# Hybrid SSD and attention layer: the two directions of the state recurrence as two lanes, with four staging tiles

## The chip, the cores and the metric

The kernel runs on one NeuronCore of a Trainium2 chip. The metric is the device time of one execution in microseconds (us), taken as the median over runs. A trace of one profiled execution stands beside the times.

## What is computed

The reference is one encoder layer over 1024 tokens of width 1024. A LayerNorm of the input `h` feeds one input projection; its columns go to two parallel groups, and an output projection with a residual LayerNorm ends the layer. The change touches the first group alone, a Mamba-2 state-space group (SSD) in two head groups `g` of 8 heads each, run forward and backward in time:

```python
def ssd_chunked(x, dt, A, Bm, Cm):          # one direction, chunks of 128 tokens
    ...
    chunk_states = jnp.einsum("bclgn,bclgjp->bcgjpn", Bm, xdt * decay_to_end[..., None])
    def step(h, inp):
        st, dec = inp
        return dec[..., None, None] * h + st, h
    _, prev = lax.scan(step, h0, ...)
    y_off = jnp.einsum("bclgn,bcgjpn->bclgjp", Cm, prev) * jnp.exp(a_cs)[..., None]
    return (y_diag + y_off).reshape(b, s, g, j, p)
...
y_fwd = ssd_chunked(xf, dtf, A_f, Bf, Cf)
y_bwd = flip(ssd_chunked(flip(xf), flip(dtb), A_b, flip(Bf), flip(Cf)))
y = y_fwd + y_bwd + D * xf
...
y_ssm = rms_norm(y * silu(z), ssm_norm_g)
```

The scan over the 8 chunks is the state recurrence. The forward and the backward one do not depend on each other; they add into the same `y`.

## The kernel before, in words

**A planner orders the work.** The kernel is written as generators, called lanes, that a class `Loom` (lines 47 to 127) runs while the program is built. Each lane issues some instructions and yields the tiles that its next instruction needs. The loom keeps a model of time for each engine: `_pe_cost`, `_dve_cost` and `_pool_cost` (lines 175 to 209) price an instruction, and `slot` (line 85) places it in the first gap of its engine's modelled calendar. `run` (line 103) resumes the lane whose tiles are ready first on that model, a margin added, and among lanes that are equally ready the one of lowest rank. Ranks and margins stand in line 29: `states=(4.4, 0.8)`, `diag=(4.125, 0.6)`, `maps=(4.4, 0.6)`, `gate=(4.375, 0.2)`, `fill=(9, 0.8)`. So the projection's matmuls (`fill`) go where nothing else is ready. TensorE's instructions keep the order in which the lanes issued them (`pinned=True`, line 227): when the model was too optimistic, TensorE waits in front of that instruction and everything behind it waits as well.

**The projection.** `fill` (line 328) takes 52 blocks of 128 columns from a queue, each of 48 matmuls of 128x512, its weights split into a high and a low part (`whi` by ScalarE, `wlo` by GpSimd, line 291). The blocks before the attention are b and c of group 0, x of group 0, z of group 0, x, b and c of group 1, z of group 1, and q, k and v of the first attention head.

**The group's lanes.** `ssd(g)` (line 697) adds four lanes. `states` (line 706) turns b into tokens, computes the products `cb`, starts the output tiles `yt` from `xt` by `start_y` (line 731, four chunks at once, the other four inside the loop), and then runs the recurrence (lines 738 to 766): backward (`d` = 1), and when all its 8 chunks are done forward (`d` = 0). One step is, in order: VectorE makes the weighted input `xw`; TensorE multiplies the state `H[d]` by c into a PSUM bank (`sb`); GpSimd decays the state, `H <- H*dec`; VectorE scales the bank into `tm`; GpSimd adds `yt <- yt + tm`; TensorE multiplies `xw` by b into another bank; VectorE adds that, `H <- H + bank`. Each group has 14 matmul pairs, 14 additions on GpSimd and 12 decays. `xw` and `tm` have two buffers each, and `tm` is shared with `tmd` (line 724) and the gate's `ys` (line 850).

`maps` (line 770) loads 16 pairs of tiles `t`, and ScalarE and VectorE (`copy_predicated`, line 797) turn each into decays; `diag` (line 804) multiplies it by `cb` on VectorE, has TensorE multiply it by `xt`, and adds the result to `yt` on VectorE. `gate` (line 824) takes a chunk when all 8 diagonal parts of its half and the forward pass of that chunk are done (`gr.fwd > c`, line 835). When the last chunk of group 0 is through, and group 1's x, b and c are there, `ssd(1)` is added; when group 1's gate is through, the attention's tiles are opened (line 972) and its lanes start.

The block c of group 1 enters the projection when `G[0].fwd == NCH` (line 863).

Of the kernel before, what the change touches and what calls it, by code (L numbers as in the profile page):

```python
# [9 lines left out]
F32 = mybir.dt.float32  # L10
# [11 lines left out]
NCH = 8  # L22
# [9 lines left out]
def col_bcast(ap, n):  # L32
    return ap.unsqueeze(len(ap.shape)).broadcast_to(list(ap.shape) + [n])
# [183 lines left out]
def hybrid_layer_kernel(  # L217
# [8 lines left out]
    loom = Loom(tc)  # L226
    T = Engine(loom, nc.tensor, "PE", _pe_cost, pinned=True)
    V = Engine(loom, nc.vector, "DVE", _dve_cost)
    A = Engine(loom, nc.scalar, "ACT", _act_cost)
    P = Engine(loom, nc.gpsimd, "POOL", _pool_cost)  # L230
# [6 lines left out]
    def open_pool(stack, name, under=(), **kw):  # L237
        return Pool(loom, stack.enter_context(tc.tile_pool(name=name, bufs=1, **kw)), under, kw.get("space") != PSUM)
# [45 lines left out]
    def stage_w(col, i, pool, bufs):  # L284
        st = pool.tile([128, 4, 128], F32, name="wst", bufs=bufs)
        return st, w_in[512 * i:512 * i + 512, col:col + 128].rearrange("(k p) n -> p k n", p=128)
# [9 lines left out]
    class Block:  # L296


        def __init__(self, col, evac, when=None, after=None):
            self.col, self.evac, self.when, self.after = col, evac, when, after  # L300
            self.w, self.begun = [], 0
            self.pair = self.last = False
# [73 lines left out]
    def sbank(shape=(128, 512)):  # L376
        return s_p.tile(shape, F32, name="sb", bufs=4)
# [3 lines left out]
    dts, acs, nacs, ef, dec, wend = [  # L381
        sp.tile([128, 2, NCH, 16], F32, name=n) for n in ("dts", "acs", "nacs", "ef", "dec", "wend")]
# [3 lines left out]
    class Group:  # L386
        def __init__(self):
            self.x_done = 0
            self.bc = {}
            self.z_done = 0  # L390
            self.fwd = 0
            self.diag = [0, 0]
            self.gate = self.started = 0
            self.prepared = False
            self.q = []

    G = [Group(), Group()]
# [45 lines left out]
    def bc_block(g, name, when=None):  # L443
        def after(dst):
            G[g].bc[name] = dst
            return
            yield
        conv_block((8 if name == "b" else 10) + g, when,
                   lambda: sp.tile([128, S], F32, name=name + "_ch"), after)
# [33 lines left out]
    with tc.tile_pool(name="dp", bufs=1) as dp_, tc.tile_pool(name="p0", bufs=1) as p0_:  # L483
# [178 lines left out]
        for i in range(2):  # L662
            for b in queue[:2]:
                st, src = stage_w(b.col, i, p0, 4)
# [29 lines left out]
    yl = late["yl"] = open_pool(sx, "yl", (dp, p0))  # L694
    sq = late["sq"] = open_pool(sx, "sq", (dp, p0))

    def ssd(g):
        gr = G[g]
        hs = slice(8 * g, 8 * g + 8)
        cb = []  # L700
        env = {}

        def heads(t):
            return t.rearrange("p (h e) -> p h e", h=8)

        def states():
            yield lambda: gr.x_done == 4 and len(gr.bc) == 2
            xt, b_ch, c_ch = gr.xt, gr.bc["b"], gr.bc["c"]
            b_tok = yl.tile([128, NCH, 128], F32, name="b_tok")
            yt = env["yt"] = [yl.tile([128, 4, 512], F32, name=f"yt{h}") for h in range(2)]  # L710
            H = [yl.tile([128, 512], F32, name=f"H{d}") for d in range(2)]
            yield from to_tokens(b_ch, lambda half, pt: A.copy(b_tok[:, 4 * half:4 * half + 4, :], pt))
            dg = yl.tile([128, NCH], F32, name="dg")
            dc = yl.tile([128, NCH, 8], F32, name="dc")
            for half in range(2):
                pt = bank((128, 4, 128))
                yield (c_ch, pt)
                for j in range(4):
                    t = slice(128 * (4 * half + j), 128 * (4 * half + j) + 128)
                    T.matmul(pt[:, j, :], b_ch[:, t], c_ch[:, t], start=True, stop=True)  # L720
                m = yl.tile([128, 4, 128], F32, name="cb", bufs=2)
                A.copy(m, pt)
                cb.append(m)
                tm = sq.tile([128, 4, 128], F32, name="tmd", tag="tm", bufs=2)
                V.tensor_mul(tm, pt, ident.unsqueeze(1).broadcast_to([128, 4, 128]))
                V.tensor_reduce(dg[:, 4 * half:4 * half + 4], tm, axis=mybir.AxisListType.X, op=ALU.add)
            gr.prepared = True
            V.tensor_mul(dc, dts[:, 1, :, hs], col_bcast(dg, 8))
            V.tensor_add(dc, dc, d_skip[:, hs].unsqueeze(1).broadcast_to([128, NCH, 8]))

            def start_y(c, eng):
                eng.tensor_mul(heads(yt[c // 4][:, c % 4, :]), heads(xt[c // 4][:, c % 4, :]),
                               col_bcast(dc[:, c, :], 64))
                gr.started += 1

            for c in range(7, 3, -1):
                start_y(c, V if c % 2 else P)
            for d in (1, 0):
                order = range(NCH) if d == 0 else range(NCH - 1, -1, -1)
                for i, c in enumerate(order):  # L740
                    xc, yc = xt[c // 4][:, c % 4, :], yt[c // 4][:, c % 4, :]
                    if d == 1 and c < 4:
                        start_y(c, V if c % 2 else P)
                    if i < NCH - 1:
                        xw = sq.tile([128, 512], F32, name="xw", bufs=2)
                        V.tensor_mul(heads(xw), heads(xc), col_bcast(wend[:, d, c, hs], 64))
                    if i > 0:
                        po = sbank()
                        yield (H[d], po)
                        T.matmul(po, c_ch[:, 128 * c:128 * c + 128], H[d], start=True, stop=True)  # L750
                        efc = col_bcast(ef[:, d, c, hs], 64)
                        if i < NCH - 1:
                            P.tensor_mul(heads(H[d]), heads(H[d]), col_bcast(dec[:, d, c, hs], 64))
                        tm = sq.tile([128, 512], F32, name="tm", tag="tm", bufs=2)
                        V.tensor_mul(heads(tm), heads(po), efc)
                        P.tensor_add(yc, yc, tm)
                    if i < NCH - 1:
                        pss = sbank()
                        yield (xw, pss)
                        T.matmul(pss, b_tok[:, c, :], xw, start=True, stop=True)  # L760
                        if i == 0:
                            A.copy(H[d], pss)
                        else:
                            yield (H[d], pss)
                            V.tensor_add(H[d], H[d], pss)
                    gr.fwd += 1 - d

        order = [(1, h) for h in range(4)] + [(0, h) for h in range(8)] + [(1, h) for h in range(4, 8)]

# [54 lines left out]
        def gate():  # L824
            gz = {}

            def load(c):
                gz[c] = sq.tile([128, 512], F32, name="gz", bufs=2)
                dma(gz[c], zd[g][c])
            yield lambda: gr.z_done == 8  # L830
            load(0)
            load(1)
            for c in range(NCH):
                half = c // 4
                yield lambda: gr.diag[half] == 8 and gr.fwd > c
                y = env["yt"][half][:, c % 4, :]
                ms = sq.tile([128, 1], F32, name="ms", bufs=2)
                V.tensor_mul(y, y, gz[c])
                A.activation(gz[c], y, AF.Square, accum_out=ms)
                if c + 2 < NCH:  # L840
                    load(c + 2)
                V.tensor_scalar(ms, ms, 1.0 / 512, EPS, op0=ALU.mult, op1=ALU.add)
                P.tensor_tensor(ms, ms, mhalf, op=ALU.pow)
                yield ms
                V.tensor_scalar(y, y, ms, None, op0=ALU.mult)
                pt = bank((128, 4, 128))
                yield (y, pt)
                for b in range(4):
                    transpose(pt[:, b, :], y[:, 128 * b:128 * b + 128])
                ys = sq.tile([128, 4, 128], F32, name="ys", tag="tm", bufs=2)  # L850
                V.tensor_mul(ys, pt, col_bcast(cols[:, c_sg + 4 * g:c_sg + 4 * g + 4], 128))
                dma(y_dram[c][:, 4 * g:4 * g + 4, :], ys)
                gr.gate += 1
# [6 lines left out]
    for j in range(4):  # L860
        x_block(1, j)
    bc_block(1, "b", lambda: G[0].prepared)
    bc_block(1, "c", lambda: G[0].fwd == NCH)
    for j in range(4):
        z_block(1, j)
    ssd(0)
# [452 lines left out]
```

## Time and profile before

| | us |
|---|---|
| median of 3 runs | 1234.8 |
| lowest and highest run | 1231.69, 1235.98 |
| the profiled execution's own time | 1231.77 |
| its span from first to last instruction | 1230.1 |

Almost all instructions are recorded under line 140, the helper that every engine call goes through, so groups are told apart by the tiles that they write and read: `sb` is a bank of the states lane, `bk` a bank of everything else, `hh`, `hl`, `whi` and `wlo` belong to the projection, `xt` with `t` to the diagonal parts. PE is TensorE, DVE is VectorE, ACT is ScalarE, POOL is GpSimd. One fp32 product of 128x512 shows as two matmul rows. The recurrence of group 0 lies at 128 to 203 us of the span, that of group 1 at 300 to 376 us. Busy times in the view by stretches count time once; the sums of single durations can be larger, because successive instructions of an engine overlap at their ends.

### The profile page before, as it was taken

The numbers are of one execution on the slowest core, as the hardware profiler recorded it, in microseconds if no ns is written. First come the engines' busy times: TensorE is split into PE (matmuls) and PEld (weight loads), VectorE is DVE, ScalarE is ACT, GpSimd is POOL, SyncE is SP. The second block draws the span as 40 slices with busy tenths as digits, with TensorE's granted clock in tenths as the row PEclk, the third lists the DMA queues.
The fourth block names the chain that finished last, engine by engine and source line by source line (L and its number), as shares of the span: only waits on it lengthen the run. The fifth ranks groups of instructions, "written<-read, shape, count | busy, mean of one in ns | idle before, by whom it ended". The sixth has DMA issues, their size and how long they took to land. (4 is left out here: it accounts for less than half of the span.)

```text
span 1230.1 us, 16472 instructions
## 1 busy us (share of the span) xinstructions
PE 1173.1 (95%) x5881; PEld 920.5 (75%) x5881; DVE 898.5 (73%) x1303; ACT 701.8 (57%) x1281; POOL 471.2 (38%) x404
## 2 busy tenths in 40 slices
PE   5999999999999999999999999999999997999997
PEld 3777667788668777778787777877777776788885
DVE  6686876767876568788788887887878888762334
ACT  4557578734577466566655657556656686552221
POOL 7412564323753223323332333233232429352354
PEclk9999999999899999999999999999999999999999
DMA  6113345622344531111111121121111263023221
GB/s 199 30 36 112 86 129 158 185 64 65 94 122 144 153 113 43 28 47 48 26 48 39 43 53 26 35 52 36 43 35 43 79 210 116 26 77 121 78 86 60
DMA packets 107590, 98.02 MB, mean 80 GB/s; under 512 B 9364, under 2 KB 79349, under 8 KB 107509
## 3 DMA queue, kind: packets, MB, share of 16 engines
q1 hardware_dynamic: 107509, 96.98, 27.4%
q8 instruction: 46, 0.75, 0.3%
q14 instruction: 35, 0.29, 0.1%
HBM read 75.85 MB, written 16.91 MB: 75 GB/s over the span
## 5 line engine op out<-in xcount | busy, mean ns | idle before, releaser
L140 PE MATMUL bk<-hh,whi 128*128 128x512 f32 x832 | 352.8, 424 | 0.9 <-DVE yt L140 0.3
L140 PE MATMUL bk<-hl,whi 128*128 128x512 f32 x832 | 327.2, 393 | 3.2 <-POOL hl L140 2.8
L140 PE MATMUL bk<-hh,wlo 128*128 128x512 f32 x832 | 328.2, 394 | 0.0
L140 ACT ACTIVATE p<-p,nm 128x1024 f32<-128x1024 f32 x128 | 146.8, 1148 | 127.7 <-DVE nm L140 126.9
L140 POOL TENSOR_TENSOR wlo<-wst,whi 128x512 fp32r<-128x512 f32 x104 | 159.0, 1534 | 144.6 <-ACT whi L140 122.2
L140 POOL TENSOR_SCALAR p<-p,rs 128x1024 f32<-128x1024 f32 x56 | 64.4, 1150 | 352.7 <-DVE rs L140 293.0
L140 PEld LDWEIGHTS bk<-hh,wlo 128*128 128x128 f32 x832 | 156.7, 188 | 35.0
L140 PEld LDWEIGHTS bk<-hh,whi 128*128 128x128 f32 x832 | 157.6, 189 | 33.1 <-issue 5.7
L140 PEld LDWEIGHTS bk<-hl,whi 128*128 128x128 f32 x832 | 157.8, 190 | 32.8 <-POOL hl L140 5.5
L140 DVE CUSTOM_DVE_ANT_0 p<-sc,dist 128x1024 f32<-128x1024 f32 x128 | 151.3, 1219 | 20.2 <-PE sc L140 19.6
L140 DVE SCALAR_TENSOR_TENSOR p<-p,rs,p 128x1024 f32<-128x1024 f32 x64 | 127.7, 1995 | 21.3 <-POOL p L140 18.0
L140 ACT CAST wh<-bk 128x512 fp32r<-128x512 f32 x128 | 74.2, 580 | 50.5 <-PE bk L140 49.9
L140 DVE TENSOR_TENSOR wl<-bk,wh 128x512 fp32r<-128x512 f32 x128 | 87.1, 684 | 15.6 <-ACT wh L140 13.6
L140 ACT CAST whi<-wst 128x512 fp32r<-128x512 f32 x104 | 64.1, 621 | 42.5 <-PE bk L140 34.3
L140 PE MATMUL bk<-ident,p 128*128 128x128 f32 x512 | 78.3, 275 | 2.6 <-ACT o L140 2.2
L140 PEld LDWEIGHTS bk<-ident,p 128*128 128x128 f32 x512 | 61.0, 140 | 26.1 <-issue 5.5
L140 ACT ACT_TABLE_LOAD x46 | 59.0, 1283 | 28.9 <-DVE t L140 17.3
L140 PE MATMUL bk<-wh,vh 128*128 128x256 f32 x256 | 74.7, 292 | 0.0
L140 PE MATMUL sc<-kk,q 128*128 128x512 f32 x256 | 72.3, 394 | 0.0
L140 PE MATMUL bk<-wl,vh 128*128 128x256 f32 x256 | 72.0, 281 | 0.0
L140 PE MATMUL bk<-wh,vl 128*128 128x256 f32 x256 | 72.0, 281 | 0.0
L140 PEld LDWEIGHTS bk<-xt,t 128*128 128x128 f32 x256 | 45.0, 190 | 24.7 <-issue 16.0
(217 smaller groups left out, 2161.3 us busy)
## 6 DMA issues: line engine op xcount, KB each, us to landing
wst<-in_w_in_dram SPq DMA_DIRECT2D x104, 256.0 KB, 3.0
t<-acs_d SPq DMA_DIRECT2D x64, 256.0 KB, 3.4
ws<-in_w_out_dram SPq DMA_DIRECT2D x32, 256.0 KB, 3.8
ys<-yd SPq DMA_DIRECT2D x32, 256.0 KB, 3.0
xb<-in_x_dram SPq DMA_DIRECT2D x8, 512.0 KB, 6.5
zd<-zs SPq DMA_DIRECT2D x16, 256.0 KB, 3.0
gz<-zd SPq DMA_DIRECT2D x16, 256.0 KB, 3.1
yd<-ys SPq DMA_DIRECT2D x16, 256.0 KB, 2.8
```

The lines of the kernel that those rows point to most:

```text
L140: r = f(*args, **kw)
```

## The change

Each direction becomes a lane of its own, `chain(d, ...)`, both added to the loom under the name `states` (same rank and margin) after the four first `start_y`. A chunk's `start_y` is issued by whichever lane reaches the chunk first; the set `begun` keeps it from being issued twice, so there are still eight. `xw` and `tm` (with `tmd` and `ys`, which share its buffers) get four buffers in place of two. The gate and block c of group 1 wait for counters of both directions. Nothing is added to or taken from the arithmetic, and the lanes issue no DMA.

```diff
-            self.fwd = 0
+            self.done = [0, 0]
...
-                tm = sq.tile([128, 4, 128], F32, name="tmd", tag="tm", bufs=2)
+                tm = sq.tile([128, 4, 128], F32, name="tmd", tag="tm", bufs=4)
...
             for c in range(7, 3, -1):
-                start_y(c, V if c % 2 else P)
+                start_y(c)
             for d in (1, 0):
-                order = range(NCH) if d == 0 else range(NCH - 1, -1, -1)
-                for i, c in enumerate(order):
-                    xc, yc = xt[c // 4][:, c % 4, :], yt[c // 4][:, c % 4, :]
-                    if d == 1 and c < 4:
-                        start_y(c, V if c % 2 else P)
+                loom.add(chain(d, H[d], b_tok), "states")
+
+        def start_y(c):
+            if c in begun:
+                return
+            begun.add(c)
+            (V if c % 2 else P).tensor_mul(
+                heads(env["yt"][c // 4][:, c % 4, :]), heads(gr.xt[c // 4][:, c % 4, :]),
+                col_bcast(env["dc"][:, c, :], 64))
+            gr.started += 1
+
+        def chain(d, st, b_tok):
+
+            c_ch = gr.bc["c"]
+            order = range(NCH) if d == 0 else range(NCH - 1, -1, -1)
+            for i, c in enumerate(order):
+                xc, yc = gr.xt[c // 4][:, c % 4, :], env["yt"][c // 4][:, c % 4, :]
+                start_y(c)
+                if i < NCH - 1:
+                    xw = sq.tile([128, 512], F32, name="xw", bufs=4)
+                    V.tensor_mul(heads(xw), heads(xc), col_bcast(wend[:, d, c, hs], 64))
+                if i > 0:
+                    po = sbank()
+                    yield (st, po)
+                    T.matmul(po, c_ch[:, 128 * c:128 * c + 128], st, start=True, stop=True)
+                    efc = col_bcast(ef[:, d, c, hs], 64)
                     if i < NCH - 1:
-                        xw = sq.tile([128, 512], F32, name="xw", bufs=2)
...
+                        P.tensor_mul(heads(st), heads(st), col_bcast(dec[:, d, c, hs], 64))
+                    tm = sq.tile([128, 512], F32, name="tm", tag="tm", bufs=4)
+                    V.tensor_mul(heads(tm), heads(po), efc)
+                    P.tensor_add(yc, yc, tm)
+                if i < NCH - 1:
+                    pss = sbank()
+                    yield (xw, pss)
+                    T.matmul(pss, b_tok[:, c, :], xw, start=True, stop=True)
+                    if i == 0:
+                        A.copy(st, pss)
+                    else:
+                        yield (st, pss)
+                        V.tensor_add(st, st, pss)
+                gr.done[d] += 1
...
-                yield lambda: gr.diag[half] == 8 and gr.fwd > c
+                yield lambda: gr.diag[half] == 8 and gr.done[0] > c and gr.done[1] >= NCH - c
...
-                ys = sq.tile([128, 4, 128], F32, name="ys", tag="tm", bufs=2)
+                ys = sq.tile([128, 4, 128], F32, name="ys", tag="tm", bufs=4)
...
-    bc_block(1, "c", lambda: G[0].fwd == NCH)
+    bc_block(1, "c", lambda: G[0].done == [NCH, NCH])
```

## Rows read from the trace of the kernel before

**Rows 1.** The page's head and its first part: span, busy time by engine.

```profile
span 1230.1 us, 16472 instructions
...
PE 1173.1 (95%) x5881; PEld 920.5 (75%) x5881; DVE 898.5 (73%) x1303; ACT 701.8 (57%) x1281; POOL 471.2 (38%) x404
```

**Rows 2.** View by stretches: both recurrences, and a first stretch of each.

```profile
core 0: us, PE busy (x) PEld busy (x) DVE busy (x) ACT busy (x) POOL busy (x), PEclk, DMA share, GB/s
...
128.00:203.00 75.00, 69.67 (x306) 48.66 (x304) 62.88 (x84) 47.05 (x108) 44.66 (x34) 0.98 0.38 108
...
300.00:376.00 76.00, 70.94 (x302) 49.20 (x301) 61.75 (x81) 45.41 (x105) 47.44 (x35) 0.96 0.37 110
...
125.00:150.00 25.00, 22.85 (x107) 16.98 (x106) 22.95 (x30) 12.59 (x26) 14.43 (x11) 0.93 0.35 89
...
300.00:325.00 25.00, 22.20 (x91) 15.69 (x90) 23.04 (x30) 9.08 (x22) 15.70 (x11) 0.86 0.29 86
```

**Rows 3.** TensorE's waits in the whole span: total us, times, longest.

```profile
PE sb L140 <- DVE H L140: 6.8, 5, 2.7
...
PE bk L140 <- DVE t L140: 3.6, 4, 1.2
```

**Rows 4.** TensorE by groups, 128 to 203 us: the projection's matmuls by one of three.

```profile
L140 PE MATMUL bk<-hl,whi 128*128 128x512 f32 x43 | 17.3, 402 | 0.0
```

**Rows 5.** Timeline of TensorE, group 0, backward: products with the state.

```profile
130.40 1.02 PE L140 MATMUL sb<-H,c_ch 128*128 128x512 f32 x2
...
137.08 1.08 PE L140 MATMUL sb<-H,c_ch 128*128 128x512 f32 x2
...
144.07 1.12 PE L140 MATMUL sb<-H,c_ch 128*128 128x512 f32 x2 [2.15 <-DVE H L140]
...
152.03 1.08 PE L140 MATMUL sb<-H,c_ch 128*128 128x512 f32 x2
...
156.34 1.02 PE L140 MATMUL sb<-H,c_ch 128*128 128x512 f32 x2
```

**Rows 6.** GpSimd by groups, 128 to 203 us; two groups are left out.

```profile
L140 POOL TENSOR_TENSOR yt<-yt,tm 128x512 f32<-128x512 f32 x14 | 19.7, 1410 | 10.7 <-DVE tm L140 10.6
L140 POOL TENSOR_TENSOR H<-H,dec 128x512 f32<-128x512 f32 x12 | 14.4, 1199 | 17.1 <-PE sb L140 17.1
```

**Rows 7.** VectorE by groups, 128 to 203 us; seven groups are left out.

```profile
L140 DVE TENSOR_TENSOR t<-t,cb 128x512 f32<-128x512 f32 x13 | 13.3, 1033 | 0.1
L140 DVE TENSOR_TENSOR xw<-xt,wend 128x512 f32<-128x512 f32 x12 | 12.7, 1058 | 0.4 <-PE sb L140 0.4
L140 DVE COPY_PREDICATED t<-up_i,t 128x512 f32<-128x512 uint32 x11 | 9.7, 885 | 2.8 <-DMA t<-acs_d 2.7
...
L140 DVE TENSOR_TENSOR yt<-yt,bk 128x256 f32<-128x256 f32 x12 | 4.9, 411 | 1.7 <-POOL yt L140 1.3 <-PE bk L140 0.4
```

**Rows 8.** The tile xw: durations ns min/median/max, first and last start.

```profile
L140 DVE TENSOR_TENSOR xw<-xt,wend x28: 675/1148/1759, 125.6 to 361.1; 128x512 f32<-128x512 f32 x28
```

**Rows 9.** Timeline, 142 to 146 us: VectorE's same operation alone and beside GpSimd.

```profile
142.13 0.71 DVE L140 COPY_PREDICATED t<-up_i,t 128x512 f32<-128x512 uint32 x1
...
145.27 1.45 POOL L140 TENSOR_TENSOR H<-H,dec 128x512 f32<-128x512 f32 x1 [0.51 <-PE sb L140]
...
145.74 1.57 DVE L140 COPY_PREDICATED t<-up_i,t 128x512 f32<-128x512 uint32 x1
```

**Rows 10.** The tile H: durations ns min/median/max.

```profile
L140 POOL TENSOR_TENSOR H<-H,dec x24: 1041/1058/1517, 131.5 to 368.8; 128x512 f32<-128x512 f32 x24
L140 DVE TENSOR_TENSOR H<-H,sb x24: 664/675/689, 136.1 to 371.5; 128x512 f32<-128x512 f32 x24
```

**Rows 11.** The tile yt: GpSimd's additions, durations ns min/median/max.

```profile
L140 POOL TENSOR_TENSOR yt<-yt,tm x28: 1263/1292/1747, 135.6 to 374.7; 128x512 f32<-128x512 f32 x28
```

More of the change, by code (lines that the diff above doesn't have):

```diff
@@ L701, in ssd @@
         env = {}
+        begun = set()
         def heads(t):
@@ L713, in states @@
             dg = yl.tile([128, NCH], F32, name="dg")
-            dc = yl.tile([128, NCH, 8], F32, name="dc")
+            dc = env["dc"] = yl.tile([128, NCH, 8], F32, name="dc")
             for half in range(2):
@@ L729, in states @@
             V.tensor_add(dc, dc, d_skip[:, hs].unsqueeze(1).broadcast_to([128, NCH, 8]))
[L731 to L734, printed above, removed]
             for c in range(7, 3, -1):
-                start_y(c, V if c % 2 else P)
+                start_y(c)
             for d in (1, 0):
-                order = range(NCH) if d == 0 else range(NCH - 1, -1, -1)
-                for i, c in enumerate(order):
-                    xc, yc = xt[c // 4][:, c % 4, :], yt[c // 4][:, c % 4, :]
-                    if d == 1 and c < 4:
-                        start_y(c, V if c % 2 else P)
-                    if i < NCH - 1:
-                        xw = sq.tile([128, 512], F32, name="xw", bufs=2)
[L746 to L766, printed above, removed]
```

## The prediction

> **What bounds the kernel now.** I read the page's first part, then the waits, then the stretches of the two recurrences, then the groups of the engines inside them. TensorE is busy for 1173.1 of 1230.1 us [rows 1]: no schedule that keeps its work can win more than what it loses to idling and to a lower clock. The profiled execution took 1231.77 us by its own time, 3.0 us under the median of 1234.8; the sums below are made against its own time, and those 3.0 us are added at the end.
>
> Where the change acts, TensorE is idle 75 - 69.67 = 5.3 us in group 0's recurrence and 76 - 70.94 = 5.1 us in group 1's [rows 2]. In the first stretch of each, the granted clock is 0.93 and 0.86 of full speed, a mixture of the two levels 2.4 and 1.2 GHz, and comes after the longest of these waits; 25 x 0.07 = 1.75 and 25 x 0.14 = 3.5 us of work are lost that way. So 7.1 us are lost in the one and 8.6 us in the other, 15.6 us together. The waits name the reason: 6.8 us for VectorE's update of the state, 3.6 us for its part of the diagonal tiles [rows 3].
>
> The recurrence does not hold TensorE up by its length. The projection fills the room: 43 of each of its three kinds of matmul run between 128 and 203 us [rows 4]. A shorter chain is worth nothing by itself here; the work that it frees is only exchanged for projection work. TensorE loses time only where an instruction that the planner put next is not ready. So the question is not how long the recurrence lasts but whether VectorE and GpSimd keep up with the planner's order. They hardly do: VectorE is busy for 22.95 and 23.04 of 25 us in the first stretches [rows 2], and it is just there that the waits are.
>
> **The change part by part.** It removes no arithmetic and adds none: 14 products with the state, 14 additions, 12 decays and 8 `start_y` a group stay. No DMA is issued or moved by the lanes; SyncE's queue sees the same loads of `t` and stores of `z`, whose places shift only with the lanes around them. The guard `begun` and the counters cost nothing on the chip, since they act while the program is built. The gate's new condition costs nothing either: the last diagonal parts come after the recurrence already, and that cover stays. Block c of group 1 waits for both directions, which end earlier than the forward one did; its place in the queue comes much later, so there is no gain in it.
>
> Four buffers for `xw` and `tm` remove waits for a free buffer. The price of those today is bounded by 0.4 us of VectorE before `xw` [rows 7] in group 0, off TensorE's path as long as the products wait for the state instead. I take 0 for it, with 0.4 a group as the other end.
>
> The two lanes are the step that counts. First, how dense the planner will make the recurrence. Undisturbed steps of one chain stand 156.34 - 152.03 = 4.3 us apart; the first ones, with the `start_y` among them, 6.7 and 7.0 us [rows 5]. Two chains side by side need on GpSimd, per pair of steps, two decays and two additions, 2 x (1.06 + 1.29) = 4.7 us at the medians [rows 10, 11]. Six such intervals are 28.2 us, the slower beginning adds 2 x 2.2, the step before the first product 2.4 and the one after the last 4.7: 39.7 us. GpSimd's whole work in the stretch is 44.7 us [rows 2] (its two great parts are 19.7 and 14.4 [rows 6]). I take 45 us for what was 75.
>
> Second, what VectorE has to do in those 45 us. Its work for the diagonal tiles is 13.3 + 9.7 + 4.9 = 27.9 us in 75 [rows 7], and keeps its pace, since it hangs on its own lanes: 27.9 x 45/75 = 16.7. The rest of its 62.9 us [rows 2], 35.0, belongs to the recurrence and its preparation and all falls into the 45. That makes 51.7 us of work in 45, so VectorE is 6.7 us late by the end. Its operations will not stay as short as that, either. `xw` takes 0.675 us at best, 1.148 in the median and 1.759 at worst [rows 8]. What stretches it is GpSimd: the same `copy_predicated` took 0.71 us with GpSimd quiet and 1.57 us when it began 0.47 us after a decay; it ended 0.59 us after that decay did [rows 9], so it had waited for it and then run. The update of the state, which reads a PSUM bank, stays within 664 and 689 ns [rows 10]. With GpSimd busy for most of the stretch in place of 60% (44.66 of 75), I add a quarter of a microsecond to every other one of the 12 `xw` and of the (13 + 11) x 0.6 = 14 diagonal operations in the 45 us, 13 x 0.25 = 3.3 us: 10 us late.
>
> The ends of that term: with all of these operations at their shortest (0.68 us, and 0.71 for the predicated copy) the recurrence's part falls by 12 x 0.38 = 4.6 to 30.4, the diagonal part by 13 x 0.35 + 11 x 0.17 = 6.4 to 21.5, of which 12.9 lie in the 45 us; 43.3 us fit, and nothing is late. With them at their longest (1.76 and 1.57) the parts are 35.0 + 12 x 0.70 = 43.4 and (27.9 + 13 x 0.54 + 11 x 0.69) x 0.6 = 25.5: 24 us late. I take 10, near the durations that today's first stretches show.
>
> Third, what of it TensorE sees. It runs in program order, so a product that waits for a state holds up the projection behind it, and with it the evacuations on ScalarE. The planner's margin of 0.8 us covers the first of the lateness, and 9 us are left. For the lower clock after such waits I take 2.5 us, the mean of today's 1.75 and 3.5, between 0 and 3.5. A stretch then loses 11.5 us, both lose 23, and today's 15.6 go: **+7.4 us**. 1231.8 + 7.4 + 3.0 = 1242. The ends: -15.6 (nothing lost, 1219) and 2 x (24 + 3.5) - 15.6 = +39 (1274).
>
> After the recurrence, VectorE and GpSimd have less to do than today, and the waits for `t` there shrink; they are within the 15.6 already.
>
> **The rivals.** *The waits vanish (faster).* While one chain is with GpSimd the planner has the other chain, the diagonal parts and the projection to put in front, so each product could come later than its state. For it: of 24 updates of a state only five were waited for, and the longest wait was 2.7 us [rows 3, 10]. It decides if VectorE's lateness L stays below 6 us a stretch (L - 0.8 + 2.5 under 15.6/2); two thirds of the 15.6 us won is 10 us, 1225, and all of it 1219. Against it: the lateness arises where the work is densest, and the change makes it denser.
>
> *GpSimd and VectorE take turns (much slower).* If every operation of VectorE with two SBUF operands excludes every one of GpSimd, as [rows 9] shows for one pair, their times add. GpSimd's 44.7 us holds some waiting; with the median in place of the mean for decays and additions (1.20 to 1.06 and 1.41 to 1.29) it is 41.3. To that come 12 `xw` at 0.68 and six tenths of 13 products and 11 copies at 0.68 and 0.71, 8.2 + 10.0: 59.5 us of work in 45, 14.5 late. TensorE loses 14.5 - 0.8 + 2.5 = 16.2 a stretch, +17 us in all: 1252. It decides if GpSimd, not VectorE, is the last one that the state's update waits for. The Trainium skill ("SBUF — State Buffer", section "SBUF: two separate sides") says the same of the whole class: GpSimd and VectorE share one pair of ports, held for a full instruction, and the other engine blocks. By that rule this rival's 1252 would be the forecast, and without any sharing the lower end above; rows 9 agree with it for one instruction, and no row shows the queues under both chains. I leave it a chance of its own because part of the delay falls on additions to `yt` that nobody waits for at once.
>
> *Nothing happens (same).* The two lanes have the same rank and margin; if the planner's GpSimd calendar spaces them to some 55 us, VectorE's work is 35.0 + 20.5 = 55.5 and the lateness is like today's: 1235. That is also where the change would not do what it says, should the chains follow each other in practice.
>
> **How the numbers follow.** The forecast (VectorE late, TensorE waiting) has 0.40, with a range of its own of 1239 to 1250; the turns of GpSimd and VectorE 0.15; no change 0.15; the vanishing waits 0.30. A measurement of this kernel can tell about 0.3% (3.7 us) from nothing. Faster by more than that is 0.30, within it 0.15, slower 0.55. The range has to take in most of the faster case and the turns: 1223 to 1262 leaves out the best part of the one (0.07) and what is left towards 1274 (0.07).
>
> **What would show it.** Right: the recurrences shrink from 75 us to about 55 to 60 with the waiting included; VectorE busy for over 90% there, and GpSimd near it; the mean `xw` over 1.2 us; TensorE's waits for the state's update at 15 us or more in place of 6.8; the granted clock below 1 in both stretches; after them, up to the gates, TensorE fuller than today; the attention unchanged. Wrong: waits for the state at 4 us or less and a clock of 1.00 in both stretches would mean the faster rival, and a mean `xw` as today with longer waits would mean that the sharing is not what stretches the chain. A change of the attention's own waits by more than 3 us would mean that the planner's new order reaches further than I thought.

## The result and the profile after

The changed kernel takes 1242.97 us (median of 5 runs, 1239.96 to 1246.61), the kernel before 1234.14 in the same comparison. The ratio is 1.0074, with a 95% interval of 1.0049 to 1.010: about 9 us slower, clear of the 0.3%. The forecast was 1242, with 0.55 for slower.

The page of the changed kernel's profiled execution, its head and first part:

```profile
span 1238.1 us, 16462 instructions
...
PE 1175.4 (95%) x5881; PEld 923.2 (75%) x5881; DVE 894.0 (72%) x1303; ACT 700.4 (57%) x1280; POOL 478.5 (39%) x404
```

Against [rows 1] the span is 8.0 us longer, and TensorE is busy for only 2.3 us more: the rest is idling. Where it lies, the view by stretches tells, first of the kernel before, cut at the same times:

```profile
124.00:205.00 81.00, 75.67 (x349) 54.12 (x348) 64.65 (x86) 52.83 (x118) 46.12 (x36) 0.98 0.40 112
205.00:300.00 95.00, 91.55 (x459) 75.89 (x458) 67.22 (x78) 55.24 (x117) 26.95 (x31) 1.00 0.39 116
300.00:378.00 78.00, 72.62 (x312) 50.40 (x311) 62.49 (x82) 46.63 (x108) 47.44 (x35) 0.96 0.36 108
378.00:440.00 62.00, 59.12 (x294) 47.45 (x294) 35.44 (x63) 33.30 (x66) 16.09 (x18) 1.00 0.54 163
```

and of the changed one, with six of its stretches of 25 us behind, for the clock and for VectorE (the columns are those of [rows 2]):

```profile
124.00:205.00 81.00, 72.09 (x329) 50.68 (x327) 62.12 (x86) 48.14 (x110) 49.05 (x36) 0.98 0.36 106
205.00:300.00 95.00, 90.01 (x435) 74.47 (x434) 65.30 (x77) 55.10 (x116) 27.25 (x30) 0.96 0.42 119
300.00:378.00 78.00, 67.92 (x304) 47.28 (x303) 61.15 (x81) 41.02 (x98) 48.14 (x34) 0.98 0.34 94
378.00:440.00 62.00, 61.48 (x315) 51.05 (x315) 31.52 (x55) 39.04 (x77) 17.25 (x18) 1.00 0.54 154
...
125.00:150.00 25.00, 20.24 (x98) 13.99 (x97) 23.34 (x32) 10.86 (x19) 16.36 (x12) 1.00 0.25 74
150.00:175.00 25.00, 20.89 (x88) 13.50 (x87) 22.91 (x31) 14.38 (x40) 20.39 (x14) 1.00 0.44 120
175.00:200.00 25.00, 24.96 (x110) 17.97 (x111) 14.90 (x24) 17.20 (x43) 8.40 (x7) 0.93 0.36 112
225.00:250.00 25.00, 20.40 (x101) 16.61 (x101) 19.88 (x30) 16.78 (x40) 9.72 (x12) 0.94 0.69 198
250.00:275.00 25.00, 25.00 (x113) 20.61 (x112) 17.00 (x15) 11.32 (x24) 7.25 (x8) 0.92 0.25 78
...
325.00:350.00 25.00, 20.25 (x73) 12.47 (x74) 21.69 (x30) 13.71 (x36) 18.16 (x14) 0.93 0.47 133
```

Subtract TensorE's busy time from the length. In the recurrence of group 0 it idles for 8.9 us in place of 5.3, in that of group 1 for 10.1 in place of 5.4. The lower granted clock after a wait costs about as much as before in the one (25 x 0.07 = 1.75 us) and less in the other (1.75 us in place of 3.5). Between them lies the gate of group 0: 1.5 us more of idling, and a clock of 0.94 and 0.92 over 50 us where it was 1.00, 3.5 us. The gate of group 1 idles 2.4 us less.

Two milestones, the same instructions in both kernels, date the loss. The timeline of TensorE, before and then after, at the transposes of group 1's b (the last thing before its recurrence):

```profile
295.15 1.04 PE L140 MATMUL bk<-ident,b_ch 128*128 128x128 f32 x8
```

```profile
302.58 1.04 PE L140 MATMUL bk<-ident,b_ch 128*128 128x128 f32 x8
```

and at the attention's score products (durations ns min/median/max, first and last start), before and after:

```profile
L140 PE MATMUL sc<-kk,q x256: 387/390/588, 427.0 to 1077.7; 128*128 128x512 f32 x128
```

```profile
L140 PE MATMUL sc<-kk,q x256: 387/390/593, 434.7 to 1085.8; 128*128 128x512 f32 x128
```

So 7.4 us are lost by the end of group 0's part and 7.7 by the start of the attention; at its last product it is 8.1. Group 1's worse recurrence is paid back at its gate.

TensorE's waits in the changed kernel:

```profile
PE sb L140 <- DVE H L140: 9.3, 3, 4.1
PE bk L140 <- DVE t L140: 5.6, 5, 2.1
...
PE bk L140 <- DVE ys L140: 4.1, 1, 4.1
PE bk L140 <- ACT zr L140: 3.9, 2, 2.4
```

The waits for the state's update are fewer and longer than in [rows 3]; those for the diagonal tiles are longer and one more. And the tiles of the recurrence (the tiles H, tm and xw; durations ns min/median/max):

```profile
L140 POOL TENSOR_TENSOR H<-H,dec x24: 1035/1466/1595, 131.4 to 359.0; 128x512 f32<-128x512 f32 x24
...
L140 POOL TENSOR_TENSOR yt<-yt,tm x28: 1262/1648/1749, 137.1 to 367.0; 128x512 f32<-128x512 f32 x28
...
L140 DVE TENSOR_TENSOR xw<-xt,wend x28: 675/747/1751, 125.5 to 352.4; 128x512 f32<-128x512 f32 x28
```

GpSimd's median decay went from 1.058 to 1.466 us [rows 10], its additions from 1.292 to 1.648 [rows 11]; VectorE's `xw` fell from 1.148 to 0.747 [rows 8]. Medians mislead here, because each group has short and long operations and the median jumps from the one kind to the other. In sums over both recurrences (120 to 400 us of the views by groups) GpSimd's additions and decays take 73.6 us in place of 68.5, and VectorE's three groups with two SBUF operands (`xw`, the products with `cb` and the predicated copies) 82.8 in place of 85.5. Two of the three, before and then after:

```profile
L140 DVE TENSOR_TENSOR t<-t,cb 128x512 f32<-128x512 f32 x32 | 29.7, 933 | 6.3 <-ACT t L140 6.2
L140 DVE TENSOR_TENSOR xw<-xt,wend 128x512 f32<-128x512 f32 x28 | 28.9, 1036 | 5.7 <-ACT xt L140 4.9 <-PE sb L140 0.8
```

```profile
L140 DVE TENSOR_TENSOR t<-t,cb 128x512 f32<-128x512 f32 x32 | 29.8, 933 | 21.1 <-ACT t L140 21.1
...
L140 DVE TENSOR_TENSOR xw<-xt,wend 128x512 f32<-128x512 f32 x28 | 25.8, 939 | 4.9 <-ACT xt L140 4.9
```

So the single operations are hardly longer than before, GpSimd's by 7% and VectorE's not at all; but as much work now falls into a shorter time. Between 125 and 175 us VectorE is busy for 23.34 and 22.91 of 25 us (22.95 and 19.88 before), GpSimd for 16.36 and 20.39. And the state's update, an operation of VectorE, seldom waits for GpSimd's decay itself. VectorE's waits between 124 and 205 us, before and after:

```profile
DVE H L140 <- POOL H L140: 2.1, 4, 0.7
```

```profile
DVE H L140 <- POOL H L140: 0.3, 1, 0.3
```

It stands in VectorE's own queue.

How one wait comes about can be read in the timeline around the longest one, 4.09 us:

```profile
170.52 1.49 POOL L140 TENSOR_TENSOR H<-H,dec 128x512 f32<-128x512 f32 x1
...
171.63 0.93 DVE L140 TENSOR_TENSOR t<-t,cb 128x512 f32<-128x512 f32 x1
171.97 1.71 POOL L140 TENSOR_TENSOR yt<-yt,tm 128x512 f32<-128x512 f32 x1
...
173.71 0.42 DVE L140 TENSOR_TENSOR yt<-yt,bk 128x256 f32<-128x256 f32 x1 [1.15 <-POOL yt L140]
174.04 0.68 DVE L140 TENSOR_TENSOR H<-H,sb 128x512 f32<-128x512 f32 x1
...
174.87 1.43 PE L140 MATMUL sb<-H,c_ch 128*128 128x512 f32 x2 [4.09 <-DVE H L140]
```

The decay is over at 172.0. VectorE, in its own order, makes a diagonal product first, which takes 0.93 us beside the decay (0.67 at its shortest), and GpSimd's addition takes 1.71 us beside that product (1.26 at its shortest). VectorE's next instruction needs the addition and stands for 1.15 us; only behind it comes the update of the state that TensorE has been waiting for.

### The profile page after: what moved, and what is told of

It is laid out like the page before. It is cut to its first block, busy times and chain, and to the rows that moved or that the text cites. A ratio compares the mean times of both kernels' runs of the same rounds, so it can differ in the third digit from the quotient of the medians.

```text
span 1238.1 us, 16462 instructions
## 1 busy us (share of the span) xinstructions
PE 1175.4 (95%) x5881; PEld 923.2 (75%) x5881; DVE 894.0 (72%) x1303; ACT 700.4 (57%) x1280; POOL 478.5 (39%) x404
## 5 line engine op out<-in xcount | busy, mean ns | idle before, releaser
L140 DVE CUSTOM_DVE_ANT_0 p<-sc,dist 128x1024 f32<-128x1024 f32 x128 | 151.3, 1219 | 20.2 <-PE sc L140 19.5
L140 DVE SCALAR_TENSOR_TENSOR p<-p,rs,p 128x1024 f32<-128x1024 f32 x64 | 127.3, 1990 | 21.4 <-POOL p L140 18.0
L140 ACT CAST whi<-wst 128x512 fp32r<-128x512 f32 x104 | 64.1, 621 | 49.1 <-PE bk L140 35.9
L140 PEld LDWEIGHTS bk<-xt,t 128*128 128x128 f32 x256 | 46.2, 191 | 29.6 <-issue 17.4
```

The lines of the kernel that those rows point to most:

```text
L140: r = f(*args, **kw)
```

## The experiments

Times are medians of at least 5 runs; the ratio is to the kernel before, run beside it.

**Which half of the change: lanes or tiles.** The lanes with two buffers:

```diff
-                    xw = sq.tile([128, 512], F32, name="xw", bufs=4)
+                    xw = sq.tile([128, 512], F32, name="xw", bufs=2)
...
-                    tm = sq.tile([128, 512], F32, name="tm", tag="tm", bufs=4)
+                    tm = sq.tile([128, 512], F32, name="tm", tag="tm", bufs=2)
```

(`tmd` and `ys` likewise.)

> The two lanes alone: xw, tm, tmd and ys keep two buffers. Theory (density: side by side, the two chains ask more of VectorE and GpSimd than these give, and TensorE waits): the loss is that of the lanes, so 5 to 11 us above the kernel before, like the changed kernel (+8.8 by medians). Rival (the tiles: with four buffers VectorE makes xw early, ahead of what is urgent): within 3 us of the kernel before.

The kernel before with the opposite edit, four in place of two:

> The four tiles alone, one direction behind the other as before; TensorE's order is that of the kernel before. Density: within 3 us of the kernel before. Tiles: 5 us or more above it.

The lanes alone: 1249.0 us, 1.0111 (1.0094 to 1.0128), above what I expected. The tiles alone: 1233.6 us, 0.999 (0.9978 to 1.0002), no difference. So the loss is the lanes', and larger than the changed kernel's; the tiles, worth nothing by themselves, win back some 5 us once there are two lanes (6.0 by the medians, 4.6 by the ratios). The waits of the lanes with two tiles show one that neither of the others has:

```profile
PE sb L140 <- DVE xw L140: 4.2, 2, 2.2
```

The shorter `xw` is the tiles' doing, for it shows without any lanes, in the kernel with the tiles alone:

```profile
L140 DVE TENSOR_TENSOR xw<-xt,wend x28: 675/684/1759, 125.9 to 351.9; 128x512 f32<-128x512 f32 x28
```

The longer operations of GpSimd are the lanes': its additions and decays take 74.1 us in sum with the lanes alone, 68.3 with the tiles alone.

**GpSimd's additions left out, in both kernels.** In both the line is replaced by an entry in the planner's books:

```diff
-                    P.tensor_add(yc, yc, tm)
+                    loom.note("POOL", _pool_cost("tensor_add", yc, [yc, tm]), _tiles([yc]), _tiles([yc, tm]))
```

> The changed kernel without GpSimd's 28 additions yt + tm (the contribution of the states to the output is left out); the planner still books them, so TensorE's order is unchanged. Density: with 28 x 1.5 = 42 us of GpSimd's work gone, TensorE's idle time in group 0's recurrence (8.9 us between 124 and 205 us) falls under 4 us, that in group 1's (10.1 us) under 5 us, and the time falls by 8 to 14 us against the changed kernel, to 1229 to 1235. Rival (the planner's new order is at fault elsewhere, at group 0's gate with its wait of 4.1 us and the lower clock after it): the time falls by less than 4 us.

> The kernel before without the same 28 additions (the states' contribution left out, booked by the planner as before), as a measure for the run before. Density: it has less to win, as its recurrences lose 5.3 and 5.1 us to idling; it falls by 3 to 9 us, and the difference between this pair of kernels is under 4 us where the full ones differ by 8.8. Rival (fault elsewhere): this pair differs by 6 us or more.

With lanes 1222.4 us, 0.9908 (0.9892 to 0.9924); one behind the other 1224.8, 0.9927 (0.9912 to 0.9941). Leaving them out is worth 20.5 us to the one, more than the 8 to 14 expected, and 9.4 to the other; the difference between the two is gone (2.4 us the other way round, with intervals that overlap). The same order of TensorE's work that loses 9 us loses nothing in all without these 28 instructions. The view by stretches of the kernel with lanes shows it, with 1.9 and 3.7 us of idling in the recurrences:

```profile
124.00:205.00 81.00, 79.12 (x378) 57.98 (x377) 56.41 (x90) 56.38 (x130) 28.66 (x22) 1.00 0.42 123
205.00:300.00 95.00, 90.33 (x437) 74.28 (x437) 67.58 (x80) 53.00 (x107) 28.85 (x31) 0.96 0.38 110
300.00:378.00 78.00, 74.28 (x340) 53.70 (x339) 53.58 (x84) 51.25 (x120) 26.26 (x22) 0.98 0.42 117
```

The gate of group 0 keeps its loss: 4.7 us of idling and a clock of 0.96, as in the changed kernel (5.0 and 0.96), with a wait of 3.8 us for `ys`; the transposes of group 1's b start at 293.4 us with lanes and at 291.0 without. So this part belongs to the lanes and not to the additions; group 1 makes it good in this run (the score products start at 418.3 with lanes, 420.4 without). Why the gate loses was not tried.

**What about the additions costs: their order on `yt`, GpSimd's queue, or the sharing of SBUF.** First, the additions go into a scratch tile (`scr`, made and cleared once for each group):

```diff
-                    P.tensor_add(yc, yc, tm)
+                    loom.note("POOL", _pool_cost("tensor_add", yc, [yc, tm]), _tiles([yc]), _tiles([yc, tm]))
+                    nc.gpsimd.tensor_add(env["scr"], env["scr"], tm)
```

> The changed kernel with GpSimd's 28 additions going into a scratch tile in place of yt (the states' contribution to the output is left out), booked by the planner as before. GpSimd's load is kept, but VectorE's additions of the diagonal parts to yt no longer have to wait for GpSimd's. Theory (sharing: operations of GpSimd and VectorE on SBUF hold each other up): little changes, within 4 us of the changed kernel, 1239 to 1247. Rival (order on yt: VectorE, in order, stands at an addition to yt behind GpSimd's, and the state's update behind that): falls by 8 us or more, to 1235 or less.

1240.6 us, 1.0057 (1.0042 to 1.0072). VectorE's additions to `yt` no longer depend on GpSimd's, and at most some 2.4 us are won of 20.5, which is not clear of noise (the interval overlaps that of the changed kernel, 1.0049 to 1.010): the stop of 1.15 us in the timeline above is how one wait looked, not what the loss is made of.

Then GpSimd stays as busy, but does not read SBUF:

```diff
-                    P.tensor_add(yc, yc, tm)
+                    loom.note("POOL", _pool_cost("tensor_add", yc, [yc, tm]), _tiles([yc]), _tiles([yc, tm]))
+                    for _ in range(3):
+                        nc.gpsimd.memset(tm[:, 0:432], 0.0)
```

> The changed kernel with each of GpSimd's 28 additions replaced by three memsets that together take about as long (3 x 0.45 = 1.3 us, from 0.10 us for 2 columns and 0.20 for 128) and only write SBUF (the states' contribution to the output is left out); orders of TensorE, VectorE and GpSimd as in the changed kernel. Theory (sharing: what costs is that GpSimd's and VectorE's operations that read SBUF hold each other up): most of the 20 us that leaving the additions out gave come back, 1222 to 1232, and decays fall to a median near 1.1 us. Rival (GpSimd's queue is simply too long, whatever it does with SBUF): 1238 or more.

1223.5 us, 0.9902 (0.9885 to 0.992), against 0.9908 without the additions: all that they cost is won. Its stretch, the tiles H and tm, and VectorE's products with `cb` over both recurrences (the profiled execution is the slowest of the five, 1228.6 us):

```profile
124.00:205.00 81.00, 78.54 (x374) 57.39 (x373) 56.95 (x89) 55.27 (x125) 46.21 (x64) 1.00 0.43 122
```

```profile
L140 POOL TENSOR_TENSOR H<-H,dec x24: 1041/1178/1599, 132.9 to 348.0; 128x512 f32<-128x512 f32 x24
...
L767 POOL MEMSET tm<- x84: 451/457/462, 138.5 to 357.5; 128x432 f32 x84
```

```profile
L140 DVE TENSOR_TENSOR t<-t,cb 128x512 f32<-128x512 f32 x32 | 23.2, 725 | 22.4 <-ACT t L140 22.4
```

GpSimd is busy for 46.2 us between 124 and 205, nearly the 49.1 of the changed kernel, three memsets take 3 x 0.457 = 1.37 us, between an undisturbed addition and a disturbed one, and they hardly vary. The queue is nearly as full and TensorE idles 2.5 us instead of 8.9. So it is not the length of GpSimd's queue that costs, but that its additions and VectorE's operations on SBUF hold each other up. Much of what comes back is VectorE's: its three groups with two SBUF operands take 71.3 us over both recurrences in place of 82.8.

**The other side of the sharing: VectorE's products `xw` left out, in both kernels.** TensorE multiplies `xc` in place of `xw`:

```diff
-                    V.tensor_mul(heads(xw), heads(xc), col_bcast(wend[:, d, c, hs], 64))
+                    wc = col_bcast(wend[:, d, c, hs], 64)
+                    loom.note("DVE", _dve_cost("tensor_mul", heads(xw), [heads(xc), wc]), _tiles([xw]), _tiles([xc, wc]))
```

> The changed kernel without VectorE's 28 products xw (the states are made of the unweighted input), booked by the planner as before; GpSimd's instructions are all kept. 28 x 0.6 = 17 us of VectorE go, each with two SBUF operands. Sharing: falls by 6 to 14 us, to 1229 to 1237, and GpSimd's decays and additions get shorter (median of the additions from 1.65 towards 1.3 us). Rival (GpSimd's own queue is too long, whatever VectorE does): falls by under 3 us, with GpSimd's durations near 1.6.

> The kernel before without the same 28 products xw, as a measure for the run before. Sharing and density: it falls by 2 to 6 us, less than the changed kernel does, so the pair without xw differs by under 5 us where the full pair differs by 8.8. Rival: no fall beyond 2 us.

With lanes 1232.6 us, 0.9991 (0.998 to 1.0002); without 1224.4, 0.9922 (0.9908 to 0.9936). GpSimd's operations do get short again when VectorE's go, the decays to a median of 1.16 us and the additions to their undisturbed 1.28 (in sum 69.3 us in place of 73.6):

```profile
L140 POOL TENSOR_TENSOR H<-H,dec x24: 1033/1158/1610, 131.7 to 349.6; 128x512 f32<-128x512 f32 x24
...
L140 POOL TENSOR_TENSOR yt<-yt,tm x28: 1263/1282/1787, 137.2 to 356.9; 128x512 f32<-128x512 f32 x28
```

But my expectation for the pair was wrong: the kernel before wins as much (some 9 us) as the changed one (10), and the difference of 8 us stays. Most of it lies in group 1's recurrence, here with lanes and then without:

```profile
300.00:378.00 78.00, 67.98 (x294) 47.77 (x292) 50.53 (x72) 43.62 (x105) 43.20 (x33) 0.93 0.35 104
```

```profile
300.00:378.00 78.00, 74.77 (x344) 53.69 (x343) 51.19 (x72) 53.07 (x122) 44.90 (x35) 1.00 0.43 125
```

That is 10.0 us of idling against 3.2, and a clock of 0.93 against 1.00. So lanes can lose 8 us with GpSimd's medians back to short; VectorE's products with `cb` are still stretched (a mean of 0.868 us here, 0.725 in the run with memsets). Removing 17 us of VectorE's work helps either order; of the two removals only that of GpSimd's additions brings the two orders together.

**Half as dense.** The forward lane begins when the backward one is half done:

```diff
+            if d == 0:
+                yield lambda: gr.done[1] >= 4
             order = range(NCH) if d == 0 else range(NCH - 1, -1, -1)
```

> The changed kernel with the forward lane starting when the backward one has done four of its eight chunks, so that half of the steps run side by side. Density: between the two kernels, 2 to 7 us above the kernel before. Rival (the lanes' order as such, however dense): as the changed kernel, 8 us or more above.

1264.0 us, 1.0252 (1.0229 to 1.0275), far above both kernels. The score products and the longest new wait:

```profile
L140 PE MATMUL sc<-kk,q x256: 387/393/504, 433.9 to 1111.1; 128*128 128x512 f32 x128
```

```profile
PE bk L140 <- DVE rs L140: 10.7, 3, 6.1
```

At the start of the attention this kernel is 6.9 us behind the kernel before, between the two as density has it, though hardly better than full overlap; by its last score product it is 33.4 us behind. Most of its loss thus falls in the attention, whose instructions the edit does not touch; that the planner ordered them worse is likely, and why was not tried. As a test of density it is inconclusive; it does show that an edit of the recurrence can cost more at the other end of the program than where it is made.

**A planner that knows of the sharing.** `note` books GpSimd's operations and VectorE's with two SBUF operands on a common calendar besides their own, in both kernels:

```diff
-            start = self.slot(key, start, cost)
+            start = self.slots([key, "PORT"] if port else [key], start, cost)
...
+def _port(key, op, ins):
+    n = sum(a.space != PSUM and _width(a) > 1 for a in ins)
+    return key == "POOL" or (key == "DVE" and n >= (1 if op in ("tensor_scalar", "tensor_copy") else 2))
```

(`slots` looks for the first gap that is free on all the calendars it is given.)

> The changed kernel, with a planner that books every operation of GpSimd and every one of VectorE with two SBUF operands (or a copy or scaling from SBUF) on one common calendar. Sharing: the planner then spaces the products so that fewer are late; TensorE's waits in the recurrences fall from 8.9 + 10.1 us of idling to under 12 together, 1230 to 1238. Rival (the lateness comes from something that the calendar does not hold): no fall. The planner's new order can also move the attention and the end by several us either way, so the start of the first score product is compared too.

> The kernel before with the same common calendar. Sharing: a small gain, 0 to 6 us, since its recurrences lose less; rival: no change or a loss, from a new order elsewhere.

1248.8 us for both, 1.0118 (1.0098 to 1.0137) and 1.0108 (1.0091 to 1.0125): neither wins what was expected, both lose some 12 us, and the two are equal. With lanes, the recurrences begin some 14 us later than in the changed kernel (the first product with the state at 144.4 us in place of 130.3), so their stretches are cut later here:

```profile
0.00:124.00 124.00, 102.60 (x467) 80.90 (x468) 81.52 (x117) 66.62 (x113) 48.39 (x74) 0.96 0.32 94
...
137.00:218.00 81.00, 76.94 (x341) 54.93 (x340) 57.15 (x74) 41.62 (x85) 50.80 (x38) 1.00 0.33 93
...
314.50:392.50 78.00, 73.97 (x316) 52.40 (x315) 53.01 (x70) 38.77 (x80) 49.54 (x38) 0.98 0.33 88
...
378.00:440.00 62.00, 51.22 (x246) 41.31 (x245) 36.78 (x67) 34.38 (x94) 18.68 (x17) 0.85 0.48 138
```

In the recurrences the idling is 4.1 + 4.0 us where it was 8.9 + 10.1, GpSimd's medians are 1.045 and 1.291 us, and TensorE's waits for the state's update are a single one of 2.0 us. The calendar does hold what made TensorE wait; it also spreads the chains (63.0 us from group 0's first product with the state to its last, in place of 55.8), so sharing and density are not told apart by this run. It does not pay, because the new order loses elsewhere. Before the recurrences TensorE idles for 21.4 us of the first 124, with a clock of 0.96, where the kernel before has 19.5 and 1.00. And the group's work ends later: the last projection matmul before the attention starts at 418.2 us by the timeline, group 1's gate is still at work at 446, and TensorE idles for 10.8 us between 378 and 440, with a clock of 0.85.

**The additions on VectorE.**

```diff
-                    P.tensor_add(yc, yc, tm)
+                    V.tensor_add(yc, yc, tm)
```

> The changed kernel with the 28 additions yt + tm on VectorE in place of GpSimd. 28 x 0.6 = 17 us go to VectorE, 42 us leave GpSimd. By the runs so far leaving the additions out gave 20.5 us, and 17 us of VectorE's products were worth 10 us: 1243 - 20 + 10 = 1233, range 1228 to 1238. Rival (VectorE is the bound): 1243 or more.

1236.5 us, ratio 1.0006 (0.9994 to 1.0018): the loss of the lanes is gone, as the sum of the earlier runs had it. It computes the whole layer and equals the kernel before; no version here that computes the whole layer is clearly faster than that.

## Why the prediction was right

**What bounds the kernel** held: the pair of chains is over sooner (from first to last product with the state 55.8 us in group 0, 130.3 to 186.1, in place of 69.5) and that bought nothing.

**The loss per stretch** was forecast at 11.5 us and measured at 8.9 + 1.75 = 10.7 in group 0 and 10.1 + 0.07 x 25 = 11.8 in group 1 (the clock between 325 and 350 us is 0.93). Against 7.1 and 8.9 in the same cuts of the kernel before that is +6.5 us, for +7.4 forecast.

**The cause inside it** held in its main step and failed in one term. VectorE is late where the work is densest, as forecast: it is busy for 92% of the time between 125 and 175 us, and GpSimd, which was to come near that, for 74%. That GpSimd's additions and VectorE's operations on SBUF hold each other up is what the runs without the additions and with memsets show. But the term "its operations get longer still", 3.3 us of the 10, was wrong: the mean of `xw` in group 0's stretch was to pass 1.2 us and was 1.11, nearly the 1.06 of [rows 7], and the three groups together got no longer (82.8 us for 85.5); what got longer was GpSimd's work, by 5.1 us over both groups. The forecast had named a mean `xw` as today with longer waits as a sign that sharing is not what stretches the chain. That sign came, and it misled: VectorE's operations were already stretched in the kernel before, and the lanes pressed them into less time. Without the 3.3 the forecast's own sum would have been 6.7 - 0.8 + 2.5 = 8.4 us a stretch, +1.2 us in all, 1236. So the nearness of 1242 to 1243 is in part luck.

**The waits** for the state's update were to reach 15 us; they came to 9.3. The rest of the idling in the recurrences stands before other instructions: the diagonal tiles 5.6 us, z's staging 3.9. That these lie behind the same delays is likely and was not shown.

**The tiles at 0** were right for the kernel before (0.999) and wrong in the lanes, where they are worth some 5 us. The lanes alone lose 15 by the medians, twice what the sum gave them; the forecast of the two together met the result partly because this term and that of the lanes were off in opposite directions.

**The gates** were not in the sum. At group 0's, 1.5 us of idling and about 3.5 us of clock came on top; at group 1's, 2.4 us came back. Together that is +2.6 us that the forecast had at nothing; with the 6.5 of the recurrences it makes 9.1, near the 8.0 of the spans. The attention kept its length (650.7 us from first to last score product before, 651.1 after), as forecast; the run with half the overlap shows that this was no certainty.

**The rivals.** That GpSimd and VectorE hold each other up the runs bear out, for the operations of GpSimd that read SBUF; but the rival's own condition, that the state's update waits for GpSimd last, did not come true (0.3 us of such waits in group 0's stretch), and its price, 16.2 us a stretch, was too high by five. In its words every operation of GpSimd excludes VectorE's. The Trainium skill ("SBUF — State Buffer", section "SBUF: two separate sides") has VectorE's two-operand operations excluded only against an operation of GpSimd that reads SBUF. The run with memsets agrees: at 46.2 us of GpSimd's work the loss was gone. That the waits vanish was wrong for the kernel as it is; with the additions left out the two lanes lose nothing against one behind the other.

## What to carry to other kernels

Two independent chains side by side are over sooner than one behind the other, but where other work fills every gap of the bounding engine that is worth nothing, and density is a price. In this kernel GpSimd's and VectorE's operations that read SBUF hold each other up, so take their times with both engines busy, not the shortest ones, before believing that they run in parallel. A planner that prices engines one by one packed the chains too tightly here. Compare sums as well as medians when durations are of two kinds. And when an edit changes a planned order, date the loss by milestones, since it can appear far from the edit.

## What was not expected of the hardware

Three memsets of 0.457 us each on GpSimd, together longer than an undisturbed addition, cost TensorE next to nothing (1223.5 us against 1222.4 with nothing in their place), where the additions cost 20 us: the memsets' durations are 451 to 462 ns over 84 of them, beside 1262 to 1749 for the additions. And a good part of their price fell on the other engine: with memsets in their place VectorE's products with `cb` fell from a mean of 0.933 to 0.725 us, over both recurrences.
